# Products with the identity between TensorE's first modulation products and ahead of a retention chunk's value products

## The chip, the cores and the metric

The kernel runs on one core of a Trainium2 chip. The metric is the device time of one execution in microseconds (us); smaller is better. Of several runs the median is given. The core has five engines with a queue of their own each: TensorE (PE; its weight loads are shown as PEld), VectorE (DVE), ScalarE (ACT), GpSimd (POOL) and SyncE (SP), which only starts transfers. The profile also gives the clock that was granted to TensorE: 1.00 is its upper level (2.4 GHz), about 0.5 its lower one (1.2 GHz).

## The reference

A trunk of two layers (DEPTH 2) over 512 latent tokens and 256 context tokens of 1024 features. Everything is float32.

```python
for l in range(DEPTH):
    mod_x = (silu(c) @ ada_w[l] + ada_b[l])[:, None, :]       # modulation, latent
    mod_y = silu(c_ctx) @ ada_w[l] + ada_b[l]                 # modulation, context
    shx1, scx1, gx1, shx2, scx2, gx2 = jnp.split(mod_x, 6, axis=-1)
    ...
    hx = rms_norm(x, norm1_g[l]) * (1.0 + scx1) + shx1
    hy = rms_norm(y, norm1_g[l]) * (1.0 + scy1) + shy1
    mx, my = token_mixers(hx @ w_in[l], hy @ w_in[l], ...)
    x = x + gx1 * (mx @ w_out[l])
    hx = rms_norm(x, norm2_g[l]) * (1.0 + scx2) + shx2
    x = x + gx2 * swiglu(hx, ffn_w1[l], ffn_w3[l], ffn_w2[l])
    ...
return rms_norm(x, final_norm_g)
```

`token_mixers` splits the columns of the input projection over four groups of heads. The one that matters here is retention: it works on chunks of 128 tokens, in both directions. A chunk's output is (scores of its queries and keys, times a table of decays) times its values, plus its decayed queries times a state that is carried from chunk to chunk.

## The kernel before, in words

Tokens come in six tiles of 128: tiles 0 to 3 are latent, 4 and 5 context, and the order of work is 4, 5, 0, 1, 2, 3. A long float32 product is computed as three products of split operands (`mm3`: the rounded part times the rounded part, rounded times rest, rest times rounded), one PE instruction each at one column per cycle; these are lines L467 to L469 of the profile. ScalarE makes the rounded part of a weight (`split_unit`, L449), VectorE or GpSimd the rest (`sub_lo`, L213). Products of plain float32 (the modulation at the start, transpositions, all of retention) are shown as two instructions each.

**Order.** The program is written in loops, and a scheduler that works with modelled durations puts each engine's instructions into an order of its own; within an engine they run in that order. SyncE's transfers stand in one queue, in order. So an instruction that waits holds up all behind it on its engine. `tc.high_priority()` lets the scheduler put instructions forward.

**Start.** `c` and `c_ctx` are loaded, transposed on PE (`pu_87`, L745), and go through silu into `sT` (shown as `cth`, L746). `ada_load` (L314) loads eight tiles of the modulation weights, 128 x 512 each, into tiles `a` (tag `a0`), which rotate among a few buffers: a load waits for the products that read the tile which was in its buffer. `ada_first(q)` multiplies them for a quarter `q` of the features (L326, `po_174`), and the result goes through a copy (L329) and two transpositions (L332) into the modulation vectors. `norm_stats` (L479 to L486: ScalarE squares, VectorE reciprocal root and scaling) normalizes a tile of tokens, `norm_T` transposes it (L507, into `pt`), applies the modulation (L514, VectorE) and splits it (ScalarE L515, then L213). Then come the first products of the input projection (L467 to L469), whose weights `raw` come at L459 on SyncE's queue. The tokens' own loads (L725: tiles `b` and `ldr`) stand on the same queue.

**Retention.** In `ret_proj` a block of projections (`nat_block`, into PSUM `pg`) yields gate and values; per tile, VectorE multiplies in the decays (L1222, `rt`), PE forms the update of the state (L1226, `pu`), ScalarE copies it out (L1228), and VectorE runs the recurrence of the states in 64 x 64 pieces (L1246). `ret_chunk(t)` then transposes queries and keys (L1257), ScalarE copies them (L1259, `qT`), GpSimd decays the queries (L1262), PE forms the scores (L1267), VectorE multiplies them by the decay table (L1270, tiles `P`), and PE adds into one PSUM tile `po` the products with the states (L1278) and with the values (L1282). The first chunk is tile 4 in layer 0, and tile 0 in layer 1, where only latent tiles are done. The scheduler weaves the chunks into the next block of projections, 416 columns wide (L467 to L469 with 128x416).

PSUM tags: `g` (2 buffers), `u` (1), `s` (3), `t` (1), `o` (1); in the profile the tiles are named `pg`, `pu`, `ps`, `pt`, `po` after the variable or the tag.

Of the kernel before, what the change touches and what calls it, by code (L numbers as in the profile page):

```python
# [16 lines left out]
P = 128  # L17
# [70 lines left out]
def build(tc, I, out, opts=None):  # L88
    opts = merged(opts)
    nc = tc.nc  # L90
    pe, act, dve, pool, sp = nc.tensor, nc.scalar, nc.vector, nc.gpsimd, nc.sync
# [71 lines left out]
    NT_ = (opts or {}).get("nt", {1: ("s", "t", "o"), 2: ("t", "o")})  # L163
    HF = (opts or {}).get("hf", "ldq")
    RA = (opts or {}).get("ra", 3)
    WU = (opts or {}).get("wu", "PT")
    PF = {1440: 2, 2464: 2, 416: 2, 928: 2, 0: 9}
    PF.update((opts or {}).get("pf", {}))
# [12 lines left out]
    def PS(tag):  # L181
        uid[0] += 1
        st = site(tag)
        return pp.tile([P, 512], F32, tag="p" + st, name=f"p{tag}_{uid[0]}", bufs=SPB.get("p" + st, PSB[tag]))
# [31 lines left out]
    ident = C("ident", [P, P])  # L216
# [66 lines left out]
    def rsqrt1(a, nm):  # L283
# [7 lines left out]
            dve.scalar_tensor_tensor(y, u, c, y, op0=ALU.add, op1=ALU.mult)  # L291
        return y


    mod_d = [DT(f"mod_d{l}", [2, 6 * D]) for l in range(LAYERS)]
    modT = [C(f"modT{l}", [P, 2, 4, 8]) for l in range(LAYERS)]
# [21 lines left out]
    def ada_first(q, ws):  # L318

        ps = PS("o")[:, 0:256]  # L320
        for k in range(8):
            w = ws[k]
            for vi in range(2):
                g = 2 * vi + k % 2
                with tc.high_priority():
                    pe.matmul(ps[32 * g:32 * g + 32, :], sT[:, k, :], w[:, vi], start=(k < 2), stop=(k > 5),  # L326
                              tile_position=(0, 32 * g))
        rt = T("rt", [P, 256])
        act.activation(rt, ps, AF.Copy)  # L329
        pt = PS("o")[:, 0:256].rearrange("p (a b) -> p a b", a=2)  # L330
        for b in range(2):
            pe.transpose(pt[:, b, :], rt[:, b * P:(b + 1) * P], ident)  # L332
        half_ = S("adah", 8, bufs=2).rearrange("p (a b c) -> p a b c", a=2, b=2)
        even, odd = (pt.rearrange("p b (v e x) -> p v e x b", v=2, e=2)[:, :, e, 0:2, :] for e in range(2))
        m = modT[0].rearrange("p s v k -> p v s k")[:, 0:2, :, 2 * q:2 * q + 2]
        dve.tensor_copy(half_, odd)
        dve.tensor_tensor(half_, even, half_, op=ALU.add)
        i, r = VROW["b0"]
        bias = vecs[i][:, r:r + 16].rearrange("p (v o k) -> p v o k", v=2, o=1)[:, :, :, 2 * q:2 * q + 2]
        dve.tensor_tensor(m, half_, bias.to_broadcast([P, 2, 2, 2]), op=ALU.add)  # L340
        dve.scalar_tensor_tensor(m[:, 1], m[:, 1], 1.0, vec("g1_0", 2 * q, 2).unsqueeze(1).to_broadcast([P, 2, 2]),
                                 op0=ALU.add, op1=ALU.mult)
# [468 lines left out]
    for l in range(LAYERS):  # L811
# [360 lines left out]
        def ret_proj():  # L1172
# [77 lines left out]
            def ret_chunk(t):  # L1250
# [13 lines left out]
                for e in range(2):  # L1264
                    ps = PS("s")
# [3 lines left out]
                    for d in range(2):  # L1269
                        dve.tensor_tensor(at[d][:, e::2, :], ps[:, 0:256].rearrange("p (h b) -> p h b", h=2),  # L1270
                                          Dm[d][:, e::2, :], op=ALU.mult)
                po = PS("s")
                first = {4: 0, 5: 1}.get(t)
                for d in range(2):
                    cross = first != d
# [59 lines left out]
        if l == 0:  # L1335
            blks = {}

            def parts(q):
                W = load_nat(w_in, 1952, 512, range(2 * q, 2 * q + 2))
                if q == 0 and XO == 0:  # L1340
                    load_xres(x_in, range(4))
                if q < 3:
                    A0[q + 1] = ada_load(q + 1)
                if q == 0 and XO == 1:
                    load_xres(x_in, range(4))
                ada_first(q, A0.pop(q))
                for p in (2, 0, 1):
                    if q == 0:
                        blks[p] = [norm_stats(t, inplace=True) for t in (2 * p, 2 * p + 1)]
                    norm_T(0, 1, p, blks[p], hT, (2 * q,), ("t",))  # L1350
                return W

        na_attn = na_proj()
# [184 lines left out]
```

## Time and profile before

| what | value |
|---|---|
| median of 3 runs | 1909.32 us (1909.04 to 1910.92) |
| the profiled execution's own time | 1910.68 us |
| its span | 1908.8 us |
| mean granted clock of TensorE | 0.985 |
| PE busy | 1811.7 us, 95% |
| VectorE busy | 1187.5 us, 62% |
| ScalarE, GpSimd busy | 35%, 32% |

The profiled execution is 1.36 us over the median, and 1.9 us of its time lie outside its span. PE's busy time counts products at either level of the clock alike: a product that takes twice as long at the lower level is busy twice as long.

### The profile page before, as it was taken

How to read it: one execution, taken by the hardware profiler on the slowest of the kernel's cores; microseconds unless marked ns; L12 is line 12 of the kernel's file. 1: busy time of each engine (PE TensorE's matmuls, PEld its weight loads, DVE VectorE, ACT ScalarE, POOL GpSimd, SP SyncE). 2: the span in 40 equal slices, each digit the busy share in tenths (PEclk: the TensorE clock that was granted, in tenths of full speed). 3: DMA queues.
4: the chain of work that ended last, by engine and by line, in shares of the span. 5: the costliest groups of instructions: out<-in, count | busy, mean ns of one | idle time of the engine just before them, and what ended most of it. 6: DMA issues, size and time to landing. Idle time of an engine off the chain costs nothing. (4 is left out here: it accounts for less than half of the span.)

```text
span 1908.8 us, 28192 instructions
## 1 busy us (share of the span) xinstructions
PE 1811.7 (95%) x10447; PEld 1494.0 (78%) x10447; DVE 1187.5 (62%) x2676; ACT 672.9 (35%) x1517; POOL 605.2 (32%) x560
## 2 busy tenths in 40 slices
PE   6899999889999999999999999899889999999997
PEld 3677777778889887888888878788777888888885
DVE  5696886877898757564434293465588863434335
ACT  3325643254542221221122233564255532222223
POOL 0211113323115443444344111211333144645542
PEclk9999999899999999999999999999999999999999
DMA  7675436445124346342222222422443033232321
GB/s 226 210 206 162 131 98 187 127 151 117 50 95 127 122 155 199 105 134 63 74 67 67 57 84 91 120 75 81 143 142 100 15 115 101 84 107 89 102 86 44
DMA packets 193555, 215.22 MB, mean 113 GB/s; under 512 B 66660, under 2 KB 141578, under 8 KB 193418
## 3 DMA queue, kind: packets, MB, share of 16 engines
q10 hardware_dynamic: 75840, 111.17, 18.8%
q1 hardware_dynamic: 117578, 102.25, 18.1%
q8 instruction: 82, 1.34, 0.3%
q14 instruction: 55, 0.45, 0.1%
HBM read 192.76 MB, written 20.63 MB: 112 GB/s over the span
## 5 line engine op out<-in xcount | busy, mean ns | idle before, releaser
L469 PE MATMUL pg<-wh,b 128*128 128x512 f32 (+2 forms) x1128 | 439.9, 394 | 7.2 <-POOL b L213 6.2
L467 PE MATMUL pg<-wh,b 128*128 128x512 f32 (+2 forms) x1128 | 443.1, 393 | 1.8 <-ACT b L515 0.9
L468 PE MATMUL pg<-wl,b 128*128 128x512 f32 (+2 forms) x1128 | 441.5, 391 | 2.2 <-DVE rs_yn L288 1.8
L467 PE MATMUL ps<-b,wh 128*128 128x512 f32 (+1 forms) x1120 | 388.2, 347 | 0.0
L469 PE MATMUL ps<-b,wl 128*128 128x512 f32 (+1 forms) x1120 | 386.7, 345 | 0.8 <-DVE wl L213 0.8
L468 PE MATMUL ps<-b,wh 128*128 128x512 f32 (+1 forms) x1120 | 386.9, 345 | 0.5 <-POOL b L213 0.5
L213 DVE TENSOR_TENSOR wl<-raw,wh 128x1024 fp32r<-128x1024 f32 (+1 forms) x131 | 207.4, 1592 | 174.9 <-ACT wh L449 145.3
L449 ACT ACTIVATE wh<-raw 128x1024 fp32r<-128x1024 f32 (+1 forms) x196 | 203.8, 1049 | 271.1 <-PE pg L469 172.3
L213 POOL TENSOR_TENSOR wl<-raw,wh 128x1024 fp32r<-128x1024 f32 (+1 forms) x65 | 160.0, 2462 | 336.7 <-ACT wh L449 286.8
L1362 POOL TENSOR_TENSOR b<-b,nat 128x512 f32<-128x512 f32 (+1 forms) x204 | 217.8, 1087 | 124.0 <-DVE nat L1360 95.0
L469 PEld LDWEIGHTS pg<-wh,b 128*128 128x128 f32 x1128 | 214.9, 191 | 49.6 <-POOL b L213 9.6
L467 PEld LDWEIGHTS pg<-wh,b 128*128 128x128 f32 x1128 | 215.5, 191 | 40.9 <-ACT b L1476 1.9
L468 PEld LDWEIGHTS pg<-wl,b 128*128 128x128 f32 x1128 | 215.2, 191 | 39.7 <-DVE rs_yn L288 2.3
L467 PEld LDWEIGHTS ps<-b,wh 128*128 128x128 f32 x1120 | 213.5, 191 | 27.4 <-issue 2.4
L469 PEld LDWEIGHTS ps<-b,wl 128*128 128x128 f32 x1120 | 213.4, 191 | 26.0 <-DVE wl L213 1.0
L468 PEld LDWEIGHTS ps<-b,wh 128*128 128x128 f32 x1120 | 213.6, 191 | 25.5 <-POOL b L213 0.7
L1360 DVE TENSOR_TENSOR nat<-pg,gate 128x512 f32<-128x512 f32 x240 | 161.9, 688 | 102.0 <-PE pg L469 97.8
L1473 ACT ACTIVATE P<-ps 128x512 f32<-128x512 f32 (+1 forms) x70 | 35.4, 505 | 224.3 <-PE ps L469 128.0
L1475 DVE TENSOR_TENSOR P<-ps,P 128x512 f32<-128x512 f32 (+1 forms) x70 | 40.1, 575 | 118.9 <-PE ps L469 118.8
L1476 ACT ACTIVATE b<-P 128x512 fp32r<-128x512 f32 (+1 forms) x70 | 37.6, 538 | 195.3 <-DVE P L1475 176.0
L397 DVE SCALAR_TENSOR_TENSOR PT<-qT,consts,PT 128x512 f32<-128x512 f32 x112 | 94.0, 857 | 14.6 <-DMA qT<-in_ada_w_dram 13.3
L213 POOL TENSOR_TENSOR b<-P,b 128x512 fp32r<-128x512 f32 (+1 forms) x24 | 27.8, 1158 | 231.9 <-ACT b L1476 231.9
(322 smaller groups left out, 2441.7 us busy)
## 6 DMA issues: line engine op xcount, KB each, us to landing
raw<-in_ffn_w_dram ACTq DMA_DIRECT2D x132, 512.0 KB
qT<-in_ada_w_dram ACTq DMA_DIRECT2D x96, 256.0 KB
raw<-in_w_in_dram SPq DMA_DIRECT2D x40, 512.0 KB
a<-in_ada_w_dram SPq DMA_DIRECT2D x32, 256.0 KB
a<-in_ada_w_dram ACTq DMA_DIRECT2D x32, 256.0 KB
xn<-in_ada_w_dram ACTq DMA_DIRECT2D x32, 256.0 KB
raw<-in_w_out_dram SPq DMA_DIRECT2D x16, 512.0 KB
ldq<-q_d SPq DMA_DIRECT2D x40, 128.0 KB
```

The lines of the kernel that those rows point to most:

```text
L213: eng.tensor_tensor(out, full, hi.bitcast(F32), op=ALU.subtract)
L397: dve.scalar_tensor_tensor(acc[s], w, sS[:, k, s:s + 1], acc[s], op0=ALU.mult, op1=ALU.add)
L449: act.activation(hi, raw_ap, AF.Copy)
L467: pe.matmul(ps, a[0], b[0], start=first, stop=False)
L468: pe.matmul(ps, a[0], b[1], start=False, stop=False)
L469: pe.matmul(ps, a[1], b[0], start=False, stop=last)
L1360: dve.tensor_tensor(tm, ps, gates[(0 if t < 4 else 2) + b], op=ALU.mult)
L1362: eng.tensor_tensor(ap, ap, tm[:, a:c], op=ALU.add)
L1473: act.activation(s1[j][:, sl], ps, AF.Silu)
L1475: dve.tensor_tensor(s1[j][:, sl], ps, s1[j][:, sl], op=ALU.mult)
L1476: act.activation(gh[j][:, sl], s1[j][:, sl], AF.Copy)
```

## The change

A helper `busy` is added, which issues `n` float32 products of a 128 x 128 stationary operand with the identity, `w` times 128 columns wide, into a PSUM tile. What they write is never read: the tile is either dropped or overwritten by the next real product with `start=True`. It is called at three places:

- in `ada_first` of the first quarter, one product of 256 columns ahead of the products of each weight tile but the first, with the tile before as the stationary operand, at high priority: 7 in all;
- after the first `norm_T` (of tiles 4 and 5): 3 products of 512 columns;
- in `ret_chunk`, into `po`, ahead of the products with states and values: 6 products of 512 columns for tile 4 in layer 0, and 3 for tile 0 in layer 1.

```diff
+    RB = ({4: 6}, {0: 3})
...
+    def busy(ps, x, n, w=4):
+
+        for _ in range(n):
+            pe.matmul(ps[:, 0:w * P].rearrange("p (a b) -> p a b", a=w), x, ident.unsqueeze(1).to_broadcast([P, w, P]),
+                      start=True, stop=True)
+
...
         ps = PS("o")[:, 0:256]
+        bz = PS("t") if q == 0 else None
         for k in range(8):
             w = ws[k]
+            if q == 0 and k:
+                with tc.high_priority():
+                    busy(bz, ws[k - 1][:, 0, 0:P], 1, 2)
             for vi in range(2):
...
                 po = PS("s")
+                busy(po, qkT[:, 2], RB[l].get(t, 0))
                 first = {4: 0, 5: 1}.get(t)
...
                     norm_T(0, 1, p, blks[p], hT, (2 * q,), ("t",))
+                    if q == 0 and p == 2:
+                        busy(PS("t"), blks[p][1][1], 3)
```

The new lines move the numbers of all lines behind them: in the rows of the changed program the new products are L298, the modulation's L337, the loads of their weights L321, `mm3` L478 to L480, the state's update L1237, the recurrence L1257, the scores L1278, the multiplication by the decays L1281, and the products with states and values L1290 and L1294. Since the scheduler orders anew, instructions also move where the program's text is the same.

TensorE at the start of the program before (names: `pu_87` is the transposition of `c`, `a_14` the first weight tile):

```order
L745 MATMUL pu_87<-consts,nat_78 128x16
L326 MATMUL po_174<-a_14_98,cth_82 32x256 x2
L241 MATMUL pu_95<-consts,nat_91 128x64
L326 MATMUL po_174<-a_15_100,cth_82 32x256 x2
L326 MATMUL po_174<-a_16_104,cth_82 32x256 x2
L326 MATMUL po_174<-a_17_106,cth_82 32x256 x2
L326 MATMUL po_174<-a_18_108,cth_82 32x256 x2
```

And after:

```order
L298 MATMUL pt_175<-consts,a_14_98 128x256
L756 MATMUL pu_87<-consts,nat_78 128x16
L337 MATMUL po_174<-a_14_98,cth_82 32x256
L242 MATMUL pu_95<-consts,nat_91 128x64
L337 MATMUL po_174<-a_14_98,cth_82 32x256
L298 MATMUL pt_175<-consts,a_15_100 128x256
L337 MATMUL po_174<-a_15_100,cth_82 32x256 x2
L337 MATMUL po_174<-a_16_104,cth_82 32x256
L298 MATMUL pt_175<-consts,a_16_104 128x256
L337 MATMUL po_174<-a_16_104,cth_82 32x256
L298 MATMUL pt_175<-consts,a_17_106 128x256
L337 MATMUL po_174<-a_17_106,cth_82 32x256 x2
```

A product with the identity now stands between each pair of tiles, and one on `a_14` at the very head of the engine's queue. Further on the three wide ones stand behind the transpositions of tile 4 and 5.

SyncE's queue, the loads from the third weight tile (`a_16`) to the first weights of the projection (`raw_144`), before, each with what it waits for (`PE_..` is a wait for TensorE, `DMAHW.._..` one for transfers):

```order
L314 DMA a_16_104<-in_ada_w_dram 128x2x256 [waits DMAHW1_49,PE_49]
L314 DMA a_17_106<-in_ada_w_dram 128x2x256 [waits DMAHW7_49,DMAHW2_49,PE_49]
L725 DMA ldr_77<-in_ctx_dram 128x256 [waits DMAHW3_49]
L314 DMA a_18_108<-in_ada_w_dram 128x2x256 [waits DMAHW4_49]
L725 DMA b_6_75<-in_ctx_dram 128x768 [waits DMAHW5_49]
L725 DMA ldr_77<-in_ctx_dram 128x256 [waits DMAHW6_49]
L314 DMA a_19_112<-in_ada_w_dram 128x2x256 [waits DMAHW1_49,PE_49]
L314 DMA a_20_114<-in_ada_w_dram 128x2x256 [waits DMAHW2_49,DMAHW0_49,PE_49]
L314 DMA a_21_116<-in_ada_w_dram 128x2x256 [waits DMAHW4_49,PE_49]
L459 DMA raw_144<-in_w_in_dram 128x2x512
```

And after:

```order
L321 DMA a_16_104<-in_ada_w_dram 128x2x256 [waits DMAHW1_49]
L321 DMA a_17_106<-in_ada_w_dram 128x2x256 [waits DMAHW2_49,PE_49]
L736 DMA ldr_77<-in_ctx_dram 128x256 [waits DMAHW3_49]
L321 DMA a_18_108<-in_ada_w_dram 128x2x256 [waits DMAHW7_49,DMAHW4_49,PE_49]
L736 DMA b_6_75<-in_ctx_dram 128x768 [waits DMAHW5_49]
L736 DMA ldr_77<-in_ctx_dram 128x256 [waits DMAHW6_49]
L321 DMA a_19_112<-in_ada_w_dram 128x2x256 [waits DMAHW1_49,PE_49]
L321 DMA a_20_114<-in_ada_w_dram 128x2x256 [waits DMAHW2_49,DMAHW0_49,PE_49]
L321 DMA a_21_116<-in_ada_w_dram 128x2x256 [waits DMAHW4_49,PE_49]
L470 DMA raw_144<-in_w_in_dram 128x2x512
```

The load of `a_16` no longer waits for TensorE and that of `a_18` now does; `raw_144` still stands behind `a_21`.

TensorE in layer 0 around the first retention chunk before (`ps_3789` is the chunk of tile 4, `ps_3851` that of tile 5, `pg_4037` a block of projections, `pu_3668` and `pu_3709` updates of the states):

```order
L469 MATMUL pg_4037<-wh_3611,b_63_238 128x416
L467 MATMUL pg_4037<-wh_3611,b_62_237 128x416
L468 MATMUL pg_4037<-wl_3612,b_62_237 128x416
L1226 MATMUL pu_3668<-rt_3665,o_3663 64x128 x4
L469 MATMUL pg_4037<-wh_3611,b_63_238 128x416
L1282 MATMUL ps_3789<-ldr_3763,P_3777 128x64
L1267 MATMUL ps_3841<-qT_3834 128x128 x2
L1267 MATMUL ps_3846<-qT_3834 128x128
L1282 MATMUL ps_3789<-ldr_3763,P_3777 128x64 x3
L1278 MATMUL ps_3789<-b_846_3718,rt_3774 128x128
L1282 MATMUL ps_3789<-ldr_3763,P_3778 128x64
L1267 MATMUL ps_3846<-qT_3834 128x128
```

And after (`ps_3801` is the chunk of tile 4, `ps_3869` that of tile 5):

```order
L298 MATMUL ps_3801<-consts,qT_3784 128x512 x3
L1237 MATMUL pu_3721<-rt_3718,o_3716 64x128 x4
L298 MATMUL ps_3801<-consts,qT_3784 128x512 x2
L1294 MATMUL ps_3801<-ldr_3775,P_3789 128x64 x4
L1290 MATMUL ps_3801<-b_848_3730,rt_3786 128x128
L1294 MATMUL ps_3801<-ldr_3775,P_3790 128x64 x2
L1290 MATMUL ps_3801<-b_848_3730,rt_3786 128x128
L1294 MATMUL ps_3801<-ldr_3775,P_3790 128x64 x2
L1278 MATMUL ps_3859<-qT_3852 128x128 x2
L1278 MATMUL ps_3864<-qT_3852 128x128 x2
L1290 MATMUL ps_3869<-b_847_3729,rt_3854 128x128
L1294 MATMUL ps_3869<-ldr_3843,P_3857 128x64
```

Behind the two scores of tile 4 one product with the identity and an update stand ahead of the first row shown, so that six of them are spread over two updates of the states. The projections `pg` have gone behind the chunk's products: seven of them follow the last row shown.

VectorE at the same place before (`P_3777`, `P_3778`: tile 4; `P_3839`, `P_3840`: tile 5):

```order
L1246 SCALAR_TENSOR_TENSOR b_846_3718<-b_846_3718,gC_3012,b_800_3444 64x64 x4
L1270 TENSOR_TENSOR P_3777<-ps_3779,b_705_2985 128x2x128
L1270 TENSOR_TENSOR P_3778<-ps_3779,b_706_2986 128x2x128
L1270 TENSOR_TENSOR P_3777<-ps_3784,b_705_2985 128x2x128
L1246 SCALAR_TENSOR_TENSOR b_845_3717<-b_843_3715,gC_3012,b_799_3443 64x64 x4
L1270 TENSOR_TENSOR P_3778<-ps_3784,b_706_2986 128x2x128
L1270 TENSOR_TENSOR P_3839<-ps_3841,b_705_2985 128x2x128
L1270 TENSOR_TENSOR P_3840<-ps_3841,b_706_2986 128x2x128
L1270 TENSOR_TENSOR P_3839<-ps_3846,b_705_2985 128x2x128
L1270 TENSOR_TENSOR P_3840<-ps_3846,b_706_2986 128x2x128
L1246 SCALAR_TENSOR_TENSOR b_844_3716<-b_846_3718,gC_3012,b_800_3444 64x64 x4
L1246 SCALAR_TENSOR_TENSOR b_844_3716<-b_844_3716,gC_3012,b_799_3443 64x64 x8
```

And after (`P_3789`, `P_3790`: tile 4; `P_3857`, `P_3858`: tile 5; `kd_13280` belongs to layer 1):

```order
L1257 SCALAR_TENSOR_TENSOR b_848_3730<-b_848_3730,gC_3024,b_802_3456 64x64 x4
L1281 TENSOR_TENSOR P_3789<-ps_3791,b_707_2997 128x2x128
L1281 TENSOR_TENSOR P_3790<-ps_3791,b_708_2998 128x2x128
L1281 TENSOR_TENSOR P_3789<-ps_3796,b_707_2997 128x2x128
L1281 TENSOR_TENSOR P_3790<-ps_3796,b_708_2998 128x2x128
L1257 SCALAR_TENSOR_TENSOR b_847_3729<-b_845_3727,gC_3024,b_801_3455 64x64 x4
L214 TENSOR_TENSOR gate_4045<-raw_4041,gate_4044 128x512
L1204 TENSOR_SCALAR kd_13280<-kd_13280 128x8
L1257 SCALAR_TENSOR_TENSOR b_846_3728<-b_848_3730,gC_3024,b_802_3456 64x64 x4
L1257 SCALAR_TENSOR_TENSOR b_846_3728<-b_846_3728,gC_3024,b_801_3455 64x64 x8
L1281 TENSOR_TENSOR P_3857<-ps_3859,b_707_2997 128x2x128
L1281 TENSOR_TENSOR P_3858<-ps_3859,b_708_2998 128x2x128
```

The multiplications of tile 5 now stand behind the whole run of the states' updates and a split of the next gate weights.

TensorE in layer 1 around the first chunk before (`ps_13842`: tile 0):

```order
L469 MATMUL pg_14094<-wh_13670,b_2209_11085 128x416
L1226 MATMUL pu_13762<-rt_13759,o_13757 64x128 x4
L467 MATMUL pg_14094<-wh_13670,b_2208_11084 128x416
L468 MATMUL pg_14094<-wl_13671,b_2208_11084 128x416
L469 MATMUL pg_14094<-wh_13670,b_2209_11085 128x416
L467 MATMUL pg_14094<-wh_13676,b_2208_11084 128x416
L468 MATMUL pg_14094<-wl_13677,b_2208_11084 128x416
L469 MATMUL pg_14094<-wh_13676,b_2209_11085 128x416
L467 MATMUL pg_14094<-wh_13676,b_2208_11084 128x416
L468 MATMUL pg_14094<-wl_13677,b_2208_11084 128x416
L1278 MATMUL ps_13842<-b_2785_13768,rt_13827 128x128
```

And after (`ps_13860`: tile 0):

```order
L1278 MATMUL ps_13850<-qT_13843 128x128 x2
L1278 MATMUL ps_13855<-qT_13843 128x128 x2
L298 MATMUL ps_13860<-consts,qT_13843 128x512
L1237 MATMUL pu_13780<-rt_13777,o_13775 64x128 x4
L298 MATMUL ps_13860<-consts,qT_13843 128x512 x2
L1290 MATMUL ps_13860<-b_2787_13786,rt_13845 128x128
L1294 MATMUL ps_13860<-ldr_13834,P_13848 128x64 x2
L1290 MATMUL ps_13860<-b_2787_13786,rt_13845 128x128
L1294 MATMUL ps_13860<-ldr_13834,P_13848 128x64 x2
```

Three products with the identity stand where nine projections stood; those have gone behind the chunk's first products.

## Rows read from the trace of the kernel before

**Rows 1.** The page, sections 1 and 2: busy time by engine, granted clock in tenths.

```profile
...
PE 1811.7 (95%) x10447; PEld 1494.0 (78%) x10447; DVE 1187.5 (62%) x2676; ACT 672.9 (35%) x1517; POOL 605.2 (32%) x560
...
PEclk9999999899999999999999999999999999999999
...
```

**Rows 2.** Windows: length, busy PE, PEld, DVE, ACT, POOL, granted clock, DMA.

```profile
...
22.90:27.20 4.30, 4.22 (x10) 3.35 (x11) 3.82 (x18) 3.33 (x11) 0.00 (x0) 1.00 0.93 326
335.20:342.40 7.20, 0.49 (x4) 0.22 (x2) 6.91 (x14) 0.62 (x3) 3.70 (x3) 0.68 0.32 90
342.40:355.60 13.20, 13.20 (x61) 11.87 (x61) 8.18 (x26) 1.47 (x3) 0.00 (x0) 0.53 0.20 67
1363.20:1372.70 9.50, 7.28 (x38) 6.52 (x38) 8.59 (x29) 0.09 (x1) 1.65 (x4) 0.82 0.01 3
1372.70:1392.40 19.70, 16.11 (x118) 14.39 (x119) 17.63 (x49) 4.97 (x9) 7.37 (x8) 1.00 0.51 161
1392.40:1399.30 6.90, 6.90 (x29) 6.77 (x29) 3.15 (x13) 1.47 (x3) 1.77 (x2) 0.51 0.58 186
...
```

**Rows 3.** Timeline of TensorE at the start: start, length, what, wait before it.

```profile
...
22.98 0.79 PE L467 MATMUL pu<-wh,b 128*128 128x512 f32 x1 [3.07 <-ACT b L515]
...
24.86 0.63 PE L469 MATMUL pu<-wh,b 128*128 128x512 f32 x1
25.28 0.63 PE L467 MATMUL pu<-wh,b 128*128 128x512 f32 x1
...
27.29 0.39 PE L468 MATMUL pg<-wl,b 128*128 128x512 f32 x1
27.52 0.39 PE L469 MATMUL pg<-wh,b 128*128 128x512 f32 x1
...
29.04 0.55 PE L507 MATMUL pt<-consts,b 128*128 128x128 f32 x3 [0.47 <-DVE b L486]
...
```

**Rows 4.** Timeline of ScalarE at the start.

```profile
...
21.48 0.84 ACT L479 ACTIVATE P<-b 128x768 f32<-128x768 f32 x1 [1.56 <-DMA b<-in_x_dram]
...
```

**Rows 5.** Lines by form, TensorE: busy, mean ns, idle time before them.

```profile
...
L326 PE MATMUL po<-a,cth 128*32 128x256 f32 x128 | 19.9, 449 | 4.8 <-DMA a<-in_ada_w_dram 4.3 <-ACT cth L746 0.3
...
```

**Rows 6.** Timeline of SyncE's DMA queue at the start.

```profile
...
6.16 1.68 SPq L314 DMA_DIRECT2D a<-in_ada_w_dram  x2
...
14.61 0.46 SPq L459 DMA_DIRECT2D raw<-in_w_in_dram  x1
...
```

**Rows 7.** Timeline of TensorE around the first retention chunk of layer 0.

```profile
...
335.20 0.45 PE L469 MATMUL pg<-wh,b 128*128 128x416 f32 x1
342.37 0.69 PE L1282 MATMUL ps<-ldr,P 128*128 128x64 f32 x2 [6.71 <-DVE P L1270]
...
355.75 0.43 PE L467 MATMUL pg<-wh,b 128*128 128x416 f32 x1
...
```

**Rows 8.** Timeline of VectorE at the same place.

```profile
...
339.69 0.41 DVE L1222 TENSOR_TENSOR rt<-nat,kd 128x256 f32<-128x256 f32 x1
...
341.89 1.09 DVE L1270 TENSOR_TENSOR P<-ps,b 128x256 f32<-128x256 f32 x3
342.89 1.16 DVE L1246 SCALAR_TENSOR_TENSOR b<-b,gC,b 64x64 f32<-64x64 f32 x4
...
350.26 3.72 DVE L1246 SCALAR_TENSOR_TENSOR b<-b,gC,b 64x64 f32<-64x64 f32 x12 [2.22 <-ACT b L1228]
...
354.62 0.68 DVE L213 TENSOR_TENSOR gate<-raw,gate 128x512 fp32r<-128x512 f32 x1
...
```

**Rows 9.** Timeline of TensorE around the first retention chunk of layer 1.

```profile
...
1363.18 0.46 PE L1278 MATMUL ps<-b,rt 128*128 128x128 f32 x2 [1.72 <-DVE b L1246]
...
1372.74 0.46 PE L1278 MATMUL ps<-b,rt 128*128 128x128 f32 x2 [2.26 <-DVE b L1246]
...
```

**Rows 10.** Timeline of VectorE there.

```profile
...
1363.69 9.53 DVE L1246 SCALAR_TENSOR_TENSOR b<-b,gC,b 64x64 f32<-64x64 f32 x28
...
```

**Rows 11.** Timeline of TensorE: four records are two float32 products of 384 columns.

```profile
...
1196.04 1.45 PE L866 MATMUL pt<-PT,xn 128*128 128x384 f32 x4
...
```

## The prediction

> **What bounds the kernel now.** The page first: PE is busy 1811.7 us, 95% of the span, VectorE 62% [rows 1]. So the kernel is as long as PE's work plus PE's pauses, some 97 us, plus what the lower clock adds to products. Next the clock: the page's row shows nines nearly everywhere [rows 1], so little is to be had from it in all; cut into windows at the places of the change, though, it is 0.53 over the 13.20 us in which PE takes up work again after the first retention chunk of layer 0 has waited, 0.82 and then 0.51 in two stretches around the first chunk of layer 1, and 1.00 between these two [rows 2]. Then PE's timeline at the three places, for what it waits for. In layer 0 PE stands still for 6.71 us up to 342.37, for VectorE's product with the decays [rows 7]; VectorE is busy 6.91 of the 7.20 us of that window [rows 2], so it is VectorE that sets the end of this pause. In layer 1 PE waits 1.72 and 2.26 us for the states' updates [rows 9], of which VectorE does 28 on end in 9.53 us [rows 10]. At the start the modulation's products wait 4.3 us for their weights [rows 5], and the first projection waits 3.07 us for ScalarE [rows 3].
>
> None of these waits is for PE. A product that nobody reads can make none of them shorter; it costs nothing inside a pause, its own length outside one, and the one thing that it can earn is a higher clock for the real products behind it.
>
> **The price of one.** Two float32 products of 384 columns take 1.45 us at the upper level [rows 11], 0.73 us each; by columns that is 0.97 us for 512 and 0.48 us for 256. At the lower level I take twice that. The 19 together are 7 x 0.48 + 12 x 0.97 = 15 us of PE at the upper level, more than any forecast below: all depends on where they fall.
>
> **Start.** Projections of 512 columns follow each other in 0.42 us at 24.86, and in 0.23 us at 27.29 [rows 3]. So up to about 27 us PE runs at half its pace, although the window's granted clock reads 1.00 [rows 2]; I go by the cadence. At that pace the seven fills cost 7 x 0.97 = 6.8 us, and 4.3 us of waits for weights take them up [rows 5]: 2.5 us over. The three wide ones cost 3 x 1.93 = 5.8 us in the wait of 3.07: 2.7 us over. At the upper pace both fit (3.4 in 4.3, 2.9 in 3.07). The ten products from 22.98 to 27.20, 4.22 us busy [rows 2], would then be done in half of it, 2.1 us sooner; but what follows waits 0.47 us at 29.04 for VectorE's scaling of the tokens [rows 3], and ScalarE begins the latent tokens only when they have landed, at 21.48 [rows 4]. That chain is behind SyncE's queue, and no fill shortens it; so I credit nothing for the warm products. The bounds here are 0 and 2.5 + 2.7 = +5.2 us.
>
> The queue matters more than PE does. Before, `a_16` is issued at 6.16 and `raw` at 14.61, behind the last of the weights [rows 6]; the latent tokens stand behind `raw`. In the new order `a_16` waits for nobody on PE and goes ahead earlier, while each later load waits for a tile that is now read by a fill too. One earlier, the others later by a fill: these about cancel while weights, not PE, are late. What remains is the first fill, at the head of PE's queue in front of the transposition of `c`: at most 0.97 us. I take half of it, **+0.5 us**.
>
> **Layer 0, first chunk.** PE leaves its work at 335.2 + 0.45 = 335.65 [rows 7]; with four projections less in front (0.2 us each at the upper level) it comes free at about 334.8. One fill, an update, three fills end at about 338. The next update waits for VectorE's `rt`, done at 339.69 + 0.41 = 340.1 [rows 8]: a pause of about 2 us is left in the middle of the fills. Two fills then lead up to 342.6, close to where VectorE's products end the pause now. So the chunk starts when it did before.
>
> What changes is the next one. Its multiplications on VectorE stood right behind those of the first chunk; now 4 updates (1.16 us), 12 more (3.72 us) and a split (0.68 us) stand ahead [rows 8]. From 343.3, where the first chunk's four multiplications end, that is 1.16 + 0.68 + 3.72 and 0.5 for small ones and the multiplication itself: ready at about 349.3. PE, if fast, has done the chunk's products and the next scores by 345.3 and then waits 4 us. Behind that are ten projections (2 us), seven value products and a state product, 3.3 us in all at the upper level, 6.6 at the lower: the same work ends at 352.6 or 355.9, against 355.75 before [rows 7]. The gain has the bounds 3.2 and 0. Were VectorE's order no limit, all of 13.20 x (1 - 0.53) = 6.2 us could come back [rows 2]; that is a rival. Which clock follows a pause of 2 us and one of 4? The rows are mixed: behind 2.26 us PE goes on at 1.00 [rows 2, 9], behind 1.72 us at 0.82, and behind 6.71 us at 0.53 [rows 2, 7, 9]. I take the middle, **-1.6 us**.
>
> **Layer 1, first chunk.** Three fills (2.9 us) take the place of nine projections (0.19 us each, 1.7 us). The chunk's state products wait for VectorE at 1363.18 as before, so a pause of some 1.5 us remains. The nine projections go behind it, and push on PE into the following pauses: 2.26 us [rows 9], and smaller ones in the 19.70 us of which PE is busy 16.11 [rows 2]. These 3.6 us can take 1.7, so I count **0**. If they don't, +1.7. If the clock stays up in the stretch at 0.51 as well, 6.90 x (1 - 0.51) = 3.4 us come back [rows 2]. It is some 30 us away from the fills, behind pauses that nobody fills, so I count none of it.
>
> **The rest.** The order also changes where the program's text does not, all through both layers' mixing stages. I read no side of it, so 0, with 2 us to either side as an allowance, by the size of PE's single pauses [rows 9].
>
> Sum: +0.5 - 1.6 + 0 + 0 = -1.1 us. Against the profiled 1910.68 that gives 1909.6, and against the median, which is 1.36 lower, 1908.2.
>
> The Trainium skill weighs against this caution. TensorE: Matmul & The Clock Gate, Part 1, "What's actually happening", says that the throttled clock is the default and that activity releases it. By that rule fills would hold the upper level, as long as they leave no long pause, and the sum would be that of rival 1. The trace agrees for the 6.71 us of rest, and doesn't settle it for two.
>
> **Rival 1, the clock stays up (faster).** The fills hold the upper level through the chunk in layer 0 and the warmer order also in layer 1. For it: both stretches at about half clock stand behind or among such pauses [rows 2, 7]. Against it: pauses of 2 and 4 us are left, and VectorE decides. Worth -3.2 and -3.4 with +0.5 at the start: -6.1, so 1903.2. If VectorE's order doesn't bind either, -6.2 in place of -3.2: 1900.2.
>
> **Rival 2, the start pays (slower).** The fills run at the lower pace and stand in front of PE's work and of the loads that wait for it. The first latent tokens land later by as much, and the whole kernel moves. It decides whether PE still runs at 0.42 us per 512 columns when the fifth weight tile (`a_18`) is used up. For it: in the trace it does so ten products later [rows 3]. Against it: PE is hardly used up to there, and the fills give it work. Worth +5.2, and with layer 0's gain at 0, 1914.5.
>
> **Rival 3, nothing.** The fills neither change the clock nor fall outside pauses: 0, 1909.3. It can't be told from the forecast by the time.
>
> **How the numbers follow.** Differences of under 0.2% (3.8 us) can't be told from none. The forecast with rival 3 has 0.49, with its own range 1906.0 to 1911.5 (bounds 0 and -3.2 in layer 0, and 2 us for the rest, rounded); rival 1 has 0.32, rival 2 0.19. The range from 1902.5 to 1913.5 leaves out the upper half of rival 2 and the extreme of rival 1. Faster: rival 1, 0.32. Slower: rival 2 without its edge, with a little for a bad order elsewhere, 0.19. Same: 0.49.
>
> **What the profile after would show.** Right, if the value products of the chunk in layer 0 start at about the same distance from the last projection as before; if PE waits some 4 us for VectorE's multiplication ahead of the next chunk; if `raw` is issued within 1 us of 14.61; and if the first latent square on ScalarE begins within 1 us of 21.48. Rival 1 would show a granted clock of 0.9 and more in the window that was 0.53, with no wait ahead of the next chunk. Rival 2 would show fills 1.9 us long for 512 columns, and 21.48 moved to 25 or so. What would make me wrong beside these: a stretch elsewhere in the mixing stages, moved by the new order, that gains or loses more than 2 us.

## The result, and the profile after

The changed kernel takes 1917.27 us (median of 7 runs, 1914.08 to 1922.36), the kernel before 1909.32; the ratio estimated from all runs is 1.0051, 95% interval 1.004 to 1.0061. It is slower, by 8 us between the medians and some 10 us by the ratio, and outside the predicted range. The profiled execution took 1916.08 us, with a span of 1914.2.

The page of after, busy time by engine and granted clock, against [rows 1]:

```profile
PE 1821.4 (95%) x10485; PEld 1493.8 (78%) x10485; DVE 1197.8 (63%) x2676; ACT 674.5 (35%) x1517; POOL 604.4 (32%) x560
...
PEclk9999999999999999999999999999999999999999
```

TensorE is busy 9.7 us more, for 38 more records (two for each of the 19 products). The slice that read 8 in the clock's row of before now reads 9: where the products were put, the clock is higher. The same windows as in [rows 2] say it in figures:

```profile
22.90:27.20 4.30, 3.85 (x16) 2.45 (x15) 3.88 (x19) 3.36 (x11) 0.00 (x0) 1.00 1.07 373
335.20:342.40 7.20, 5.95 (x16) 2.42 (x16) 6.94 (x15) 1.10 (x3) 4.01 (x3) 0.76 0.54 187
342.40:355.60 13.20, 12.47 (x90) 10.20 (x89) 11.34 (x39) 3.14 (x7) 2.75 (x3) 1.00 0.43 140
1363.20:1372.70 9.50, 7.88 (x49) 5.86 (x45) 7.21 (x22) 1.84 (x3) 4.34 (x9) 1.00 0.44 165
```

In the third window the clock is 1.00 where it was 0.53, and TensorE does 90 instructions (5 of them fills) where it did 61. The change does what its words say at the place where it was made. Its cost must lie elsewhere.

**The start.** TensorE of after (start, length, what, wait before it), against [rows 3]:

```profile
4.33 1.19 PE L298 MATMUL pt<-consts,a 128*128 128x256 f32 x2 [4.33 <-DMA consts<-in_k_ident_dram]
...
10.51 1.22 PE L298 MATMUL pt<-consts,a 128*128 128x256 f32 x2
...
12.43 0.70 PE L298 MATMUL pt<-consts,a 128*128 128x256 f32 x2
...
20.20 2.74 PE L298 MATMUL pt<-consts,b 128*128 128x512 f32 x6
23.01 0.50 PE L478 MATMUL pu<-wh,b 128*128 128x512 f32 x1
...
29.07 0.82 PE L518 MATMUL pt<-consts,b 128*128 128x128 f32 x3 [1.70 <-DVE b L497]
```

A product of 256 columns shrinks from 1.22 to 0.70 us at about 12 us: the engine runs at its full pace some 15 us earlier than before. The first projection starts at 23.01 as it did at 22.98. What the faster products win behind it is taken by the wait for VectorE, 1.70 us now and 0.47 before, and the transpositions begin at 29.07 against 29.04. SyncE and ScalarE:

```profile
15.69 0.46 SPq L470 DMA_DIRECT2D raw<-in_w_in_dram  x1
```

```profile
21.50 0.84 ACT L490 ACTIVATE P<-b 128x768 f32<-128x768 f32 x1
```

`raw` is 1.08 us later than in [rows 6], and the first latent square, 21.48 in [rows 4], hardly moves.

**The first chunk of layer 0.** TensorE of after, against [rows 7]:

```profile
332.57 0.72 PE L1278 MATMUL ps<-qT 64*128 64x128 f32 x8
336.45 2.07 PE L298 MATMUL ps<-consts,qT 128*128 128x512 f32 x2 [3.16 <-DVE nat L1227]
338.45 1.12 PE L1237 MATMUL pu<-rt,o 128*64 128x128 f32 x8
339.51 2.98 PE L298 MATMUL ps<-consts,qT 128*128 128x512 f32 x6
342.41 0.66 PE L1237 MATMUL pu<-rt,o 128*64 128x128 f32 x8
343.00 1.98 PE L298 MATMUL ps<-consts,qT 128*128 128x512 f32 x4
344.82 1.00 PE L1294 MATMUL ps<-ldr,P 128*128 128x64 f32 x8
...
348.66 0.43 PE L1294 MATMUL ps<-ldr,P 128*128 128x64 f32 x2 [0.43 <-DVE P L1281]
```

VectorE at the same place, against [rows 8]:

```profile
341.18 1.42 DVE L1281 TENSOR_TENSOR P<-ps,b 128x256 f32<-128x256 f32 x4
...
343.76 0.69 DVE L214 TENSOR_TENSOR gate<-raw,gate 128x512 fp32r<-128x512 f32 x1
...
344.44 3.71 DVE L1257 SCALAR_TENSOR_TENSOR b<-b,gC,b 64x64 f32<-64x64 f32 x12
348.18 0.76 DVE L1281 TENSOR_TENSOR P<-ps,b 128x256 f32<-128x256 f32 x2
```

A fill waits too. It writes into `po`, and the place in PSUM that `po` has here was free only when VectorE had read a projection's gate out of it (L1227, which reads a tile `pg`): 3.16 us of pause in which the product that was to fill it couldn't run. (The buffer counts given with the PSUM tags are the program's defaults. The launch line passes others, 4 for `s`, and a place can go from one tag to another, as here from `pg` to `po`.) So the first value product starts at 344.82, not at 342.37 as before. Behind it all runs at the upper level, and the second chunk waits 0.43 us for VectorE, not the predicted 4.

**Where the time went.** For each moment of before I took the moment at which after's TensorE has done as many columns of real products (float32 ones counted twice, the added ones left out). After is level at 100 us, 0.7 us ahead at 320 us, 2.6 ahead at 355, 3.2 behind at 395, 5.4 behind at 455, and 5.5 at the end. So the chunk gains about 2 us, and the next hundred microseconds, in which nothing was added, lose 8. There layer 0's latent attention runs: its compressed tokens are transposed, split by ScalarE and VectorE (`cth`, `ctl`) and multiplied. Two windows of before there, then of after:

```profile
370.00:400.00 30.00, 28.70 (x178) 25.62 (x177) 19.21 (x89) 9.84 (x32) 8.32 (x12) 1.00 0.39 126
400.00:455.00 55.00, 50.80 (x277) 41.02 (x276) 44.30 (x161) 33.82 (x96) 22.87 (x20) 0.97 0.70 191
```

```profile
370.00:400.00 30.00, 27.07 (x163) 23.69 (x163) 16.82 (x95) 10.22 (x32) 5.34 (x8) 0.94 0.28 86
400.00:455.00 55.00, 49.18 (x271) 39.26 (x270) 42.57 (x145) 31.21 (x90) 16.02 (x16) 0.94 0.60 164
```

TensorE rests 3.25 us more (5.5 of 85 us before, 8.75 after) and gets a lower clock, 0.94 for 1.00 and 0.97: estimated by length times clock, 0.06 x 30 + 0.03 x 55 = 3.5 us more. The only wait of over 1 us there before, and then the three of after:

```profile
415.49 0.44 PE L469 MATMUL po<-P,ctl 128*128 128x384 f32 x1 [2.99 <-DVE rs_yk L288]
```

```profile
373.73 0.52 PE L480 MATMUL po<-P,ctl 128*128 128x384 f32 x1 [2.40 <-DVE ctl L1083]
...
418.70 0.90 PE L1078 MATMUL po<-consts,nat 128*128 128x128 f32 x3 [2.58 <-ACT nat L1063]
...
432.36 0.64 PE L1053 MATMUL po<-consts,nat 128*96 128x128 f32 x4 [1.86 <-POOL nat L1050]
```

### The profile page after: what moved, and what is told of

Same layout as the page of the kernel before. It is cut to its first block, busy times and chain, and to the rows that moved or that the text cites. A ratio compares the mean times of both kernels' runs of the same rounds, so it can differ in the third digit from the quotient of the medians.

```text
span 1914.2 us, 28274 instructions
## 1 busy us (share of the span) xinstructions
PE 1821.4 (95%) x10485; PEld 1493.8 (78%) x10485; DVE 1197.8 (63%) x2676; ACT 674.5 (35%) x1517; POOL 604.4 (32%) x560
## 5 line engine op out<-in xcount | busy, mean ns | idle before, releaser
L480 PE MATMUL pg<-wh,b 128*128 128x512 f32 (+2 forms) x1128 | 437.7, 392 | 7.2 <-POOL b L214 5.6
L478 PE MATMUL pg<-wh,b 128*128 128x512 f32 (+2 forms) x1128 | 440.3, 391 | 2.2 <-ACT b L1336 1.4
L478 PE MATMUL ps<-b,wh 128*128 128x512 f32 (+1 forms) x1120 | 387.5, 346 | 0.0
L480 PE MATMUL ps<-b,wl 128*128 128x512 f32 (+1 forms) x1120 | 386.1, 345 | 0.7 <-DVE wl L214 0.7
L214 DVE TENSOR_TENSOR wl<-raw,wh 128x1024 fp32r<-128x1024 f32 (+1 forms) x131 | 216.7, 1663 | 172.8 <-ACT wh L460 172.4
L480 PEld LDWEIGHTS pg<-wh,b 128*128 128x128 f32 x1128 | 213.1, 189 | 50.0 <-POOL b L214 9.1
L478 PEld LDWEIGHTS pg<-wh,b 128*128 128x128 f32 x1128 | 213.7, 189 | 40.3 <-ACT b L1336 2.2
L478 PEld LDWEIGHTS ps<-b,wh 128*128 128x128 f32 x1120 | 212.9, 190 | 27.5 <-issue 2.4
L480 PEld LDWEIGHTS ps<-b,wl 128*128 128x128 f32 x1120 | 212.9, 190 | 26.1 <-DVE wl L214 0.9
L408 DVE SCALAR_TENSOR_TENSOR PT<-qT,consts,PT 128x512 f32<-128x512 f32 x112 | 88.6, 810 | 13.9 <-DMA qT<-in_ada_w_dram 12.8
```

Source lines behind the costliest of these rows:

```text
L214: eng.tensor_tensor(out, full, hi.bitcast(F32), op=ALU.subtract)
L408: dve.scalar_tensor_tensor(acc[s], w, sS[:, k, s:s + 1], acc[s], op0=ALU.mult, op1=ALU.add)
L478: pe.matmul(ps, a[0], b[0], start=first, stop=False)
L480: pe.matmul(ps, a[1], b[0], start=False, stop=last)
```

## The experiments

The theory: the six products of layer 0 made the scheduler lay out the instructions behind them anew, and that order costs, not the products. The rivals: a product costs where it runs (in the chunk, or at the start), or layer 1's part does it. Single executions of one kernel lay up to 10 us from its median (layer1_only 1917.99 against 1908.31), so verdicts rest on medians of repeated runs, and single traces are used to see what stands where.

### One part at a time

The edits, in short:

```diff
-    RB = ({4: 6}, {0: 3})
+    RB = ({}, {})          # start_only: the ten products of the start alone
+    RB = ({4: 6}, {})      # layer0_only: and no products at the start
+    RB = ({}, {0: 3})      # layer1_only: and no products at the start
```

> Only the ten products at the start; none in the retention chunks. The trace of the whole change is level with before at 100 us (0.0 us) and 0.7 us ahead at 320. Theory O (the loss comes from the new order of the instructions in layer 0): within 2 us of before, 1907 to 1910. Theory F (the products themselves cost time wherever they stand): 3 us and more slower.

Measured: 0.9995 (0.9981 to 1.0009).

> Only the six products in layer 0's first chunk; their order in this layer is that of the whole change. In its trace the lag goes from -0.7 us at 320 us to +5 us at 450. Theory O and theory F alike: 4 to 7 us slower than before, nearly the whole loss. If it is level with before, both fall and the loss lies in layer 1 or at the start.

Measured: 1.0052 (1.0035 to 1.0069), 1919.86 us: as much as the whole change.

> Only the three products in layer 1's first chunk. The trace of the whole change loses 1.9 us from 1350 to 1550 us. Theory O: 1 to 3 us slower, from layer 1's new order. Rival: within 1 us, since what is lost there is a matter of the single execution.

Measured: 1.0001 (0.9988 to 1.0013). The cost comes with layer 0's six products. Layer 1's three move about as many of TensorE's instructions in the order, in both layers, and the median is level all the same: a new order need not cost as layer 0's does.

### The order without the products, and the products without the order

A table gives the order of an engine's instructions, and an edge from each to the next holds the scheduler to it. Such an edge carries no wait of its own. An engine that isn't held is laid out anew along with those that are. In short:

```diff
+    for seq in ORDER.values():
+        for p, q in zip(seq, seq[1:]):
+            tc.add_manual_dep(ins[q], ins[p].name, edge, reason="order")
```

> The program before, held by ordering edges on TensorE, VectorE and ScalarE to the order that layer 0 has with the six products, but without them. Theory O: as slow as layer0_only or slower, 4 to 10 us slower than before, since the two microseconds that the products saved in the chunk are gone too. Theory F: level with before or faster, within 2 us, since nothing is added.

Measured: 1.0036 (1.0023 to 1.005), 1917.28 us. The kernel before, without one added product, only in the order that the six products bring about on TensorE, VectorE and ScalarE, is slower by most of the loss.

> The six products in layer 0's first chunk, all other instructions of TensorE, VectorE and ScalarE held to the order of before; the six stand right in the 6.71 us pause. Theory O: faster than before by 2 to 6 us, since the chunk behind runs at the upper clock (13.2 us at 0.53 before). Theory F: 3 us and more slower, as the pause is 6.71 us and the six take 5.8.

Measured: 0.9996 (0.9985 to 1.0006). The six products in before's order cost nothing; nor do they win the 2 to 6 us that the theory had expected there.

Then the same in halves, cut where latent attention's first transposition stands in TensorE's order. The first run has the six products and, from there on, TensorE's old order; the second has no products and, from there on, TensorE's new one.

> The six products in layer 0; the first retention chunks stand in the new order, but from the latent attention's first product of layer 0 on (the transposition that stands at 376 us in the trace before) TensorE is held to the order of before. Theory O-late (the loss comes from where the new order puts the latent attention's products): no loss, from 3 us faster to 1 us slower. Theory O-chunk (it comes from VectorE's and TensorE's order within the chunks): 4 to 8 us slower.

Measured: 1.0003 (0.9994 to 1.0011).

> No added products; TensorE stands in the old order through the first chunks of layer 0, and from the latent attention's first product on in the order that it has with the six products. Theory O-late: 6 to 9 us slower. Theory O-chunk: within 2 us of before.

Measured: 1.0054 (1.0042 to 1.0066), 1919.88 us. This last run settles the main question: no product is added, the chunk is in before's order, and the whole loss is there, with the new order behind it. Only TensorE is held to that order; VectorE's and ScalarE's follow it, up to 400 us in a few small instructions, more behind. What moved is seen in its trace. TensorE of that run (the program's lines are those of before):

```profile
368.62 0.49 PE L1067 MATMUL po<-consts,nat 128*128 128x128 f32 x3
...
374.74 0.72 PE L467 MATMUL pg<-wh,b 128*128 128x416 f32 x1 [3.62 <-DVE msm L1061]
376.46 0.69 PE L469 MATMUL po<-P,ctl 128*128 128x384 f32 x1 [1.00 <-DVE ctl L1072]
...
377.90 0.63 PE L467 MATMUL po<-gate,cth 128*128 128x512 f32 x1
```

and before:

```profile
376.07 0.49 PE L1067 MATMUL po<-consts,nat 128*128 128x128 f32 x3
...
378.77 0.44 PE L469 MATMUL po<-P,ctl 128*128 128x384 f32 x1 [0.72 <-DVE ctl L1072]
...
379.58 0.40 PE L467 MATMUL po<-gate,cth 128*128 128x512 f32 x1
```

VectorE of the run with the new order, then of before:

```profile
373.89 0.69 DVE L1294 TENSOR_TENSOR ldg<-nat,ldg 128x512 f32<-128x512 f32 x1 [1.79 <-POOL ldg L1293]
374.50 0.18 DVE L1053 COPY b<-pg 128x32 f32<-128x32 f32 x1
...
375.85 0.55 DVE L1072 TENSOR_TENSOR ctl<-po,cth 128x384 fp32r<-128x384 f32 x1
```

```profile
376.27 0.69 DVE L1294 TENSOR_TENSOR ldg<-nat,ldg 128x512 f32<-128x512 f32 x1 [1.41 <-POOL ldg L1293]
...
378.16 0.55 DVE L1072 TENSOR_TENSOR ctl<-po,cth 128x384 fp32r<-128x384 f32 x1
```

The transposition stands 26 products earlier in TensorE's order and runs 7.5 us earlier. VectorE, which still has the end of the retention chunks in front of it (the last of it, `ldg`, waits for GpSimd), comes to the split `ctl` only 2.3 us earlier. Before, projections of 416 columns filled the meantime. Now 22 of them, and four transpositions of a chunk, stand behind it, and the first projection of the next block can't start: in the program it waits until VectorE has copied the last columns of an earlier block out of its place in PSUM (L1053, right behind `ldg`; the profile names the small instruction that follows it). In before's program this block has another place, so here the order acts through the place as well. TensorE waits 3.62 us for the copy and 1.00 us for `ctl`. In layer0_order_without_products and in after a single wait for `ctl` stands there, of 2.46 and 2.40 us. Behind these waits a product of 512 columns takes 0.63 us instead of 0.40. The windows of the run with the new order:

```profile
370.00:400.00 30.00, 24.80 (x145) 21.53 (x143) 16.56 (x81) 7.58 (x24) 7.10 (x10) 0.89 0.31 103
400.00:455.00 55.00, 49.65 (x272) 40.12 (x271) 43.37 (x157) 32.60 (x96) 14.74 (x15) 0.94 0.61 172
```

Against before that is 5.05 us more rest (10.55 for 5.5) and, again estimated by length times clock, 0.11 x 30 + 0.03 x 55 = 5.0 us of clock: together about the 10 us. With the six products and the old order behind them (layer0_old_order_after_chunk) the clock there is as it was, and TensorE rests 1.46 us more:

```profile
370.00:400.00 30.00, 28.26 (x174) 25.41 (x173) 18.00 (x83) 10.07 (x32) 8.77 (x12) 1.00 0.34 110
400.00:455.00 55.00, 49.78 (x276) 41.10 (x276) 42.98 (x155) 32.30 (x91) 22.87 (x20) 0.97 0.67 187
```

### Can the products earn anything?

In the old order the fills still waited for their place in PSUM, longer than in after. TensorE of layer0_products_old_order:

```profile
339.85 7.37 PE L301 MATMUL ps<-consts,qT 128*128 128x512 f32 x12 [6.02 <-DVE nat L1227]
```

So they came at the end of the pause and ran on over it, to about 346.6. The next edit puts them into the tile that the chunk's transpositions have just left, right behind the last projection:

```diff
-                busy(po, qkT[:, 2], RB[l].get(t, 0))
+                busy(pt, qkT[:, 2], RB[l].get(t, 0))
...
+    tc.add_manual_dep(fills[0], last_projection, edge, reason="order")
+    tc.add_manual_dep(first_value_product, fills[-1].name, edge, reason="order")
```

> All in the old order, with the six products right behind the last projection ahead of the pause, and written into the chunk's transposition tile, which is free by then, instead of the tile of the values' products, for which they waited until 339.85 us. Theory C (full filling of the pause keeps the clock up in the 13.2 us behind it, and this reaches the end): 3 to 6 us faster than before, 1903 to 1906. Rival R (what is won in the chunk is taken by a later wait): within 1.5 us of before, with the lead in the trace gone by 560 us.

Measured: 0.9994 (0.9983 to 1.0005), 1906.96 us.

> TensorE, VectorE and ScalarE in the order of before in the whole program, with six products in layer 0's pause of 6.71 us and two in layer 1's pause of 1.72 us, each right ahead of the waiting product and written into the chunk's transposition tile. Theory C (the clock that is kept up behind the pauses reaches the end): 3 to 8 us faster than before. Rival R (it is taken back by waits and by falls of the clock elsewhere): within 2 us of before, as with six in layer 0 alone.

Measured: 1.0001 (0.9989 to 1.0013); here two products in layer 1 are added in the same way. In the first of the two the fills start with no wait, and the chunk's first value product at 342.80, close to before's 342.37. TensorE:

```profile
335.90 5.31 PE L301 MATMUL pt<-consts,qT 128*128 128x512 f32 x12
342.80 0.43 PE L1294 MATMUL ps<-ldr,P 128*128 128x64 f32 x2 [1.58 <-DVE P L1281]
```

and the windows of the two runs behind the fills, first layer 0 alone, then both layers:

```profile
345.00:356.00 11.00, 9.95 (x76) 8.70 (x75) 9.52 (x37) 3.36 (x8) 1.42 (x2) 1.00 0.47 145
```

```profile
345.00:356.00 11.00, 11.00 (x52) 9.94 (x50) 7.01 (x22) 1.47 (x3) 0.00 (x0) 0.53 0.17 55
```

The same order on TensorE in layer 0, with a last wait of 1.58 and 1.52 us behind the fills, once keeps the upper level and once doesn't. A gain of some 5 us in the chunk, as the first trace shows it by the reckoning above (5.2 us ahead of before at 355 us), isn't reliable, and neither median is told from no change.

### The rest of the loss

With TensorE held to the old order in layer 0 from latent attention on, the whole change should be level.

> The changed kernel with all 19 products, with TensorE held in layer 0 to the order of before from the latent attention's first product on, and nothing else changed. Theory O-late: the loss of 0.5% is gone, within 2 us of before (1907 to 1911), and the trace shows no waits of 2.4, 2.6 and 1.9 us between 370 and 440. If the start and layer 1 lose too once all stands together, 3 us and more stay.

Measured: 1.0023 (1.0012 to 1.0034). Over half of the loss is gone (0.28 of 0.51%), and 0.23% stays. The next runs look for it: layer 1's order held too (TensorE and VectorE), one part left out, or one group of the start's products.

> All 19 products; TensorE held to the old order in layer 0 from the latent attention on, and TensorE and VectorE in layer 1's retention and attention too. Theory L1 with its order as the cause: within 2 us of before. Theory L1 with the products themselves as the cause (2.9 us on TensorE ahead of a wait): 2 to 4 us slower. Theory S: 3 to 5 us slower.

Measured: 1.0029 (1.0016 to 1.0043). It isn't layer 1's order.

> As whole_change_old_late_order, but without the three products in layer 1, so that layer 1 is all in the old order. Theory L1 (the 4 us that whole_change_old_late_order has left come from layer 1, where its trace and two others lose 1.9 to 4.5 us between 1340 and 1580): within 2 us of before. Theory S (they come from the start and from the six products in the first pause, which wait for their PSUM tile): 3 to 5 us slower, as before.

Measured: 1.0016 (1.0003 to 1.003).

> The products of both retention chunks and none at the start; TensorE held to the old order in layer 0 from the latent attention on. Theory S (the start's products are what costs the rest, together with those of layer 0): within 2 us of before. Theory L1 (layer 1's products cost it): 3 to 5 us slower. If the rest is a sum of small losses of all three: 1.5 to 3 us slower.

Measured: 1.0005 (0.9996 to 1.0015).

> Of the start's products only the seven between the modulation's products, and the six in layer 0; TensorE held to the old order from the latent attention on. If the seven are what costs in theory S: 2 to 4 us slower than before. If it is the three wide ones: within 1.5 us.

Measured: 1.0025 (1.0013 to 1.0037).

> Of the start's products only the three wide ones behind the first transpositions, and the six in layer 0; TensorE held to the old order from the latent attention on. If the three are what costs in theory S: 2 to 4 us slower than before. If it is the seven: within 1.5 us.

Measured: 1.0021 (1.001 to 1.0032). The rest appears when the start's products, either group, stand together with layer 0's. Last, whether an order is behind it again: the three engines are held from the chunk itself on.

> The three wide products of the start and layer 0's six. TensorE, VectorE and ScalarE are held to before's order from the first retention chunk of layer 0 to the end of its late stage; the same products with TensorE alone held, and only from latent attention on, gave 1.0021. If what was left there came from the order in the chunk (VectorE's above all), the ratio is 1.000, within 0.001. If the start's products and layer 0's cost something together whatever the order behind them, it is 1.002 again.

Measured: 1.0023 (1.0014 to 1.0032).

> The seven products between the modulation's weights and layer 0's six, with the three engines held to before's order from the first chunk on. The same products with TensorE alone held from latent attention on gave 1.0025. The order in the chunk as the cause: 1.000, within 0.001. A cost of the two groups together: 1.002 to 1.0025.

Measured: 1.0015 (1.0005 to 1.0025).

> All 19 products, with TensorE, VectorE and ScalarE held to before's order in layer 0 from the first chunk to the end of the late stage, and TensorE and VectorE in layer 1's mixing stage. Only the start, its order up to 330 us included, is the change's own. Order alone as the cause of the slowdown: 1.000, within 0.001. Products that cost by being there, or an order ahead of 330 us that costs: 1.002 to 1.003.

Measured: 1.0025 (1.0017 to 1.0033). The order in the chunk isn't the cause of the rest: with it held, the rest stays. The trace of norm_products_layer0_old_chunk goes further: TensorE, VectorE, ScalarE and GpSimd run in before's order in the whole program, but for some 15 instructions, and 0.23% is there.

## Why the prediction was wrong

**The step that failed** is "The rest": "I read no side of it, so 0, with 2 us to either side as an allowance, by the size of PE's single pauses". One run shows layer 0's part of that term alone, and it is +0.54% (0.42 to 0.66), some 10 us. The allowance was wrong in kind: this order didn't bring one pause. It moved products ahead of work that had covered other engines' delays, the first transposition above all: after has waits of 2.40, 2.58 and 1.86 us, for VectorE, ScalarE and GpSimd, where before has one of 2.99, and by the estimate above the lower clock costs about as much as the added rest. The prediction named such a stretch as what would make it wrong. But it compared the two orders at the places of the change only; the moved transposition stands in the same two orders, some thirty microseconds behind the chunk.

**Start, +0.5:** not contradicted, -0.05% (-0.19 to +0.09) for the start alone. The two marks were met, or nearly: the first latent square moved by 0.02 us, `raw` by 1.08. The bound of +5.2 was too careful, since the early products brought the engine to its full pace at about 12 us; and, as the prediction said, the chain through VectorE and ScalarE took what that won.

**Layer 0's chunk, -1.6:** about the size that after's trace shows, but by another course, so by luck; and the medians can't tell it (0.08%) from nothing. With before's order all around, the six products gave -0.04% (-0.15 to +0.06), with the new order in the chunk and the old one behind it +0.03% (-0.06 to +0.11). The prediction had the first fill start when TensorE came free, at 334.8; it waited until 336.45 in after, and until 339.85 in the old order, for VectorE to read the tile that held its place in PSUM. The pause of 2 us among the fills was not there either: `rt` came earlier in VectorE's new order. (By the prediction's own prices one fill, an update and three fills from 334.8 end at 339, not at 338.) The wait of 4 us ahead of the next chunk was not there, 0.43 us were: the chunk's own products started 2.45 us later, so that VectorE, which began the next multiplications at 348.18, was nearly done when TensorE came to need them. The clock did rise, 1.00 for 0.53, so rival 1 saw that part rightly; what it gave back, the later start took in good part.

**Layer 1, 0:** right by the median, +0.01% (-0.12 to +0.13). In the trace of after TensorE waits longer for VectorE's states at the second chunk, where [rows 9] have 2.26:

```profile
1376.62 0.46 PE L1290 MATMUL ps<-b,rt 128*128 128x128 f32 x2 [3.95 <-DVE b L1257]
```

The 17 projections ahead of it, with those that had moved, ended at about 1372.7: they were taken up by the pauses, as the prediction had it. Even so, by the reckoning above, the six traces of kernels with the three products lose 1.9 to 4.9 us against before between 1340 and 1580 us, 3.7 on average, in either order, and the twelve of kernels with none there 0.5 on average (-0.5 to 1.9). The median's interval allows up to 2.5 us, so a small cost in layer 1 isn't ruled out.

**Rival 2** had the right sign for another reason: the start's products alone cost nothing that can be told.

The Trainium skill (TensorE: Matmul & The Clock Gate, Part 1, "What's actually happening") says that activity releases the throttled clock. After's chunk agrees, with 1.00 for 0.53; behind six fills and a last wait of 1.5 us one trace agrees and another doesn't.

**What stays open** is the 0.15 to 0.29% that remains in all eight kernels with the start's and layer 0's products together and the old order behind the chunk. Added up, the upper ends of the intervals of start_only and layer0_old_order_after_chunk reach 0.20%, so part of it may be two small costs that neither run alone can tell from nothing; in the three kernels of the eight that have layer 1's products too, those may add to it. An order can still be behind it in most of the eight, since the order ahead of 330 us and SyncE's queue were never held. By the reckoning above, the nine traces of kernels with both groups (after among them) stand on average 1.0 us behind before at 330 us, the other ten 0.1 ahead. That points to the start, but the spread of single traces is as large: start_only's own stands 2.7 us behind there, and its median is level. Tiles also get other places in memory when products are added. In layer1_only's program nearly all have others than in before, and its median is level, so that need not cost either.

## What to carry to other kernels

When a scheduler orders the program, an added instruction is two changes, itself and a new order; compare the whole order with and without it, and look hundreds of instructions behind, for a product that has moved ahead of the work which covered another engine's delay. Hold the order by edges to price the two apart: here, in layer 0, the order cost 0.5%, and the instructions nothing that could be told. A filler is an instruction with an operand, and its target must be free when the pause begins, or it starts late in the pause and runs on over its end.

## What the runs showed of the hardware

- The granted clock in a window can't be read as the pace at the start: [rows 2] give 1.00 for 22.9 to 27.2 us, where a projection of 512 columns came every 0.42 us; in after, with the same 1.00, every 0.24 us.
- The same six products with nearly the same wait behind them (1.58 and 1.52 us) left TensorE at 1.00 in the execution of one kernel and at 0.53 in that of another with the same order on TensorE up to there (345 to 356 us).
- Rest and clock came as a pair: in the run with only the order moved, 5 us of added rest between 370 and 455 us went with a clock of 0.89 and 0.94 for 1.00 and 0.97, some 5 us by the estimate above.
